# Bucket rows on TensorE for the compressed branch's biases, and a skewed read of a short line for the others

## The chip, the cores and the metric

The kernel runs on one core of a Trainium2 chip. The metric is the device time of one execution in microseconds; three executions of the kernel before took 597.0, 598.36 and 598.94 us, the median being 598.36 us. The engines are named as in the profile: PE (TensorE, with PEld for its weight loads), DVE (VectorE), ACT (ScalarE), POOL (GpSimd) and SP (SyncE, which here only issues DMAs, as SPq).

## The reference

One layer of a decoder block on a sequence of 256 positions with model width 1024: a Conformer convolution module and a sparse attention side by side, one output projection, a cross-attention into 256 memory tokens, a SwiGLU feed-forward, and RMS norms between them. What the change touches are the biases of the sparse attention. It has 16 heads of 64 and three branches: attention over 15 compressed keys (blocks of 32 positions at a stride of 16), over selected blocks, and over a window. All three add to their scores a bias that depends on the distance of query and key alone, by way of 32 buckets and one table of 32 buckets by 16 heads:

```python
dist_c = t[:, None] - c_end[None, :]
bias_c = rel_bias[t5_bucket(dist_c)].reshape(S, n_cmp, G, R).transpose(2, 3, 0, 1)
s_c = jnp.einsum("bsgrd,bngd->bgrsn", qg, k_cmp).astype(jnp.float32) * scale + bias_c
p_cmp = masked_softmax(s_c, dist_c >= 0)
```

where `c_end` of compressed key n is 16n + 31. With 256 positions the selected blocks are all four blocks of the sequence and the window covers everything, so both other branches are plain causal attention over 256 keys, each with its own keys and values, and share one bias of query minus key.

## The kernel before, in words

All weights come through one ring: `half` (L136) takes a tile of the tag "w", which has three buffers of 4 KB in each partition, has SP load 512 KB into it, and `split` (L126) writes a high part (ACT, L129) and a low part (DVE, L131) of it. When both are written, the buffer is free for the next load. A product (`product`, L146) is three matmuls on high and low parts; a `gemm` (L151) is 48 of them on two such loads, into one of two PSUM banks.

The order of the program is: norm and first cross-attention keys, the eight products u0 to u7 of the convolution module, the products kc and vc of the compressed branch, q0 to q3, ks, kw, vs, vw, a small gate product wg, the gates ga0 to ga3, then eight calls of `pair` (L517), one for each two heads, with the products gc0 to gc3 and v0 to v3 as fillers between them, and then output projections, cross-attention and feed-forward.

Beside these run the 31 taps of the depthwise convolution, made at a lower priority (L323 to L330): `taps_g` on ACT and POOL (L317 to L321), `taps_v` on DVE (L304). When they are all there, `layer_norm_sums` (L597) adds them up on POOL, and PE makes the mean `mu` (L604) from that.

The order of instructions within an engine, the place of every DMA in SP's queue and the buffer that a tile takes are settled before the run by a planner, which plays the program through with a model of its own and gives each engine the ready instruction of the highest priority. `tc.issue_after(ins)` adds that the instructions of its block stand behind `ins` in an issue order; it is no wait for `ins` to end.

The biases before: `relt` (L333, a "w" tile) holds the bucket table and, for 383 distances, which bucket each has; one product gives `rel_ps`, a line of 384 bias values (negated) for each head, copied to `rel_sb` (L338, 16 partitions). `table` (L343) writes 8 query rows of `negb`, a table of 16 heads by 128 queries by 256 in DRAM, straight from `rel_sb` by an access that steps back one element for each query. Its 16 calls stand behind the products kc, vc, q0 to q3, ks and kw. `bias_of` (L348) loads two heads of `negb`, 256 KB, into a tile of the tag "nb" (two buffers). It is called eight times for the compressed branch, as `nbc` (L490), and eight times for the pairs, as `nb` (L520).

The compressed branch makes its scores `cs_ps` (L482) in high and low columns, ACT copies the high ones to `nsc` (L485), DVE adds the low ones (L486), sets the columns that no query sees (L488), and adds the biases, every 16th column of each `nbc` tile, in 16 small additions (L493). Minimum, subtraction, exponential (L500, queued behind the sigmoid of ga3), mask, sum and scaling follow, and four transposes (L511). `nsc` is a tile of the tag "pr" (four buffers), which `rel_sb`, `zz` and the pairs' `p1` tiles take too.

`xr` (L688) is a second load of x, 1 MB, for the residual after the output projection at 329 us; its buffer was that of `zin` of the product vc.

Of the kernel before, what the change touches and what calls it, by code (L numbers as in the profile page):

```python
# [25 lines left out]
BUCKETS = 32  # L26
MAX_DIST = 128
EPS = 1e-6
BIG = 1e30
NCMP = 15  # L30
# [27 lines left out]


@with_exitstack  # L60
def tile_hybrid_block(
# [9 lines left out]
    cp: bass.AP,  # L71
    rel: bass.AP,
    out: bass.AP,
):
    nc = tc.nc
# [18 lines left out]
    def small(name, shape, dt=F32, tag=None, bufs=1):  # L94
        return sb.tile(shape, dt, tag=tag or name, name=name, bufs=bufs)
# [4 lines left out]
    def aux(name, shape, tag, bufs):  # L100
        return axp.tile(shape, F32, tag=tag, name=name, bufs=bufs)
# [147 lines left out]
    for at, n in ((0, 2), (2, 2), (4, 2), (6, 2)):  # L249
        hs = slice(at, at + n)  # L250
# [58 lines left out]
    def taps_g(j, begin):  # L309

        y = yt[:, j:j + 2]
        for t in range(begin, TAPS):
# [7 lines left out]
            if t > begin:  # L320
# [11 lines left out]

    relt = small("relt", [P, 512], tag="w", bufs=3)  # L333
    nc.sync.dma_start(relt, rel)
    rel_ps = aux("rel_ps", [P, 384], "s", 2)
    nc.tensor.matmul(rel_ps, lhsT=relt[:, 0:P], rhs=relt[:, P:512],
                     start=True, stop=True)
    rel_sb = small("rel_sb", [HEADS, 384], tag="pr", bufs=4)  # L338
    nc.scalar.activation(rel_sb, rel_ps[:HEADS], AF.Copy)
    negb = drp.tile([HEADS, P, S], F32, name="negb")  # L340
    row = rel_sb[:]

    def table(i):  # L343

        nc.sync.dma_start(negb[:, 8 * i:8 * i + 8], bass.AP(tensor=row.tensor, offset=row.offset + P - 1 - 8 * i,
                                                            ap=[list(row.ap[0]), [-1, 8], [1, S]]))

    def bias_of(hp, name):  # L348

        t = small(f"{name}{hp}", [P, 2, S], tag="nb", bufs=2)  # L350
        nc.sync.dma_start(t, negb[2 * hp:2 * hp + 2].rearrange("h q k -> q h k"))
        return t
# [7 lines left out]
    for kv, name in enumerate(("kc", "vc")):  # L360
        ps = gemm(name, h)
        for i in range(2):
            table(2 * kv + i)
        kc = long(f"{name}t", 11 + 2 * kv, (P, GROUPS, S))
# [47 lines left out]
    for j in range(4):  # L412
        ps = gemm(f"q{j}", h)
        for i in range(2):
            table(4 + 2 * j + i)
# [12 lines left out]
    for br, name in enumerate(("ks", "kw")):  # L428
        ps = gemm(name, h)
        for i in range(2):  # L430
            table(12 + 2 * br + i)
        for lo, g in ((0, 0), (64, 1)):
# [46 lines left out]

    nsc = small("nsc", [P, 2, HEADS, 16], tag="pr", bufs=4)  # L480
    for qb in range(2):
        cs_ps = aux(f"cs_ps{qb}", [P, HEADS, 2, 16], "s", 2)  # L482
        for hd in range(HEADS):
            nc.tensor.matmul(cs_ps[:, hd], lhsT=qh(hd, qb), rhs=kcp[:, hd // 4], start=True, stop=True)
        nc.scalar.activation(nsc[:, qb], cs_ps[:, :, 0], AF.Copy)  # L485
        nc.vector.tensor_tensor(out=nsc[:, qb], in0=cs_ps[:, :, 1], in1=nsc[:, qb], op=ALU.add)  # L486
    for qb, n in ((1, NCMP), (0, 7)):
        nc.vector.memset(nsc[:, qb, :, n:], BIG)  # L488
    for hp in range(8):
        nb = bias_of(hp, "nbc")  # L490
        hs = slice(2 * hp, 2 * hp + 2)
        for qb, off, n in ((1, 31, NCMP), (0, 159, 7)):
            nc.vector.tensor_tensor(out=nsc[:, qb, hs, 0:n], in0=nsc[:, qb, hs, 0:n],  # L493
                                    in1=nb[:, :, off::16][:, :, 0:n], op=ALU.add)
    mc = small("mc", [P, 2, HEADS])
# [21 lines left out]
    def pair(hp):  # L517
        heads = (2 * hp, 2 * hp + 1)
        g = heads[0] // 4
        nbp = bias_of(hp, "nb")  # L520
        s0 = aux(f"s0_{hp}", [P, 2, 2, P], "s0", 1)
# [166 lines left out]
    xr = long("xr", 14)  # L688
    nc.sync.dma_start(xr, xt)
    x1, xg, acc1 = residual(by_halves([f"wo{j}" for j in range(4)], (yh, yl)), xr, PP_GX, "1", (0, 1, 6))  # L690
# [106 lines left out]

def _buckets():

    half = BUCKETS // 2  # L800
    ratio = MAX_DIST // half
    res = []
    for n in range(S):
        if n < half:
            res.append(n)
            continue
        b = half
        while b < BUCKETS - 1 and n ** half >= half ** half * ratio ** (b + 1 - half):
            b += 1
        res.append(b)  # L810
    return res


_OUTS = [((P, NB, S), "float32")]
# [88 lines left out]
```

## Time and profile before

| what | value |
|---|---|
| median of three executions | 598.36 us |
| the profiled execution's own time | 597.25 us |
| its span | 595.5 us |
| granted TensorE clock, mean | 0.984 |
| PE, DVE, ACT, POOL busy | 94%, 75%, 64%, 30% of the span |
| bytes moved by DMA | 101.48 MB |

The span is the time from the first to the last instruction of the profiled execution; the 1.75 us between it and the execution's time lie around it. A row of a timeline holds the start in us, the duration in us, engine, line of the source, operation, tile written and tile read, and a count where several were merged (the duration is then that from the first to the last). "[x <-Y]" at its end says that the engine sat idle x us before it and that Y ended the wait. A row of the view of waits has the waiting engine and instruction, what it waited for, and then the microseconds in total, how often, and the longest. A row of the stretches has start and end, length, and each engine's busy time with its instructions, then the granted clock, the share of time that the DMA engines were busy, and GB/s.

### The profile page before, as it was taken

What the parts mean: (1) busy time and instruction counts of PE and PEld (TensorE: products, weight loads), DVE (VectorE), ACT (ScalarE), POOL (GpSimd) and SP (SyncE); (2) the same over time, 40 slices, a digit from 0 to 9 for tenths busy, and PEclk for the clock granted to TensorE, in tenths of its full rate; (3) what the DMA queues carried; (4) which work ended last, traced back from release to release, by engine and by line L of the source; (5) the groups of instructions that cost most, each with busy time, mean ns of one, the idle gap of its engine ahead of it and who ended that gap; (6) DMA issues with size and microseconds to landing.
All of it is one profiled execution on the core that took longest, in us unless ns stands there. A gap on an engine that the chain in (4) does not pass through costs nothing.

```text
span 595.5 us, 11133 instructions
## 1 busy us (share of the span) xinstructions
PE 561.8 (94%) x4248; PEld 531.5 (89%) x4248; DVE 447.5 (75%) x807; ACT 382.1 (64%) x712; POOL 177.8 (30%) x127
## 2 busy tenths in 40 slices
PE   8999895969899889999999999999999999999995
PEld 7889895969899889888999999998888888899995
DVE  5585798889999999977675957577877877854542
ACT  5557686377775789969844666467666566554440
POOL 0344997688799934000000300041000000000000
PEclk9999999898899999999999999999999999999998
DMA  8755568763577535321355554145556556566631
GB/s 291 244 181 176 197 179 194 200 222 105 147 232 236 194 114 187 123 85 68 126 180 188 180 166 153 66 153 182 204 176 210 179 177 210 177 176 184 191 89 70
DMA packets 34789, 101.48 MB, mean 170 GB/s; under 512 B 3632, under 2 KB 11184, under 8 KB 34480
## 3 DMA queue, kind: packets, MB, share of 16 engines
q1 hardware_dynamic: 33008, 98.67, 51.6%
q10 hardware_dynamic: 1728, 2.10, 1.3%
q8 instruction: 33, 0.54, 0.3%
q14 instruction: 20, 0.16, 0.1%
HBM read 96.56 MB, written 3.15 MB: 167 GB/s over the span
## 4 chain that ended last, share of the span: by engine, by line
PE 64%; DVE 15%; DMA 7%; issue 6%; ACT 5%; POOL 3%; DVEq 0%; SPq 0%; ACTq 0%; POOLq 0%
PE ps_f L745 14%; PE ps_f L747 7%; DVE yp L304 4%; PE fo L149 4%; PE fo L148 4%; PE fo L147 4%; DMA q<-in_wst_dram 3%; DMA k<-in_wst_dram 2%; PE ps_xq L148 1%; PE ps_pw L148 1%; PE ps_xo L148 1%; PE ps_v L149 1%; PE ps_xq L147 1%; PE ps_xq L149 1%; PE ps_xo L147 1%
## 5 line engine op out<-in xcount | busy, mean ns | idle before, releaser
L321 POOL TENSOR_TENSOR yt<-yt,vw 128x512 f32<-128x512 f32 x69 | 113.3, 1643 | 34.0 <-ACT vw L319 29.9
L319 ACT ACTIVATE vw<-vt,ppt 128x256 f32<-128x256 f32 x114 | 51.0, 499 | 23.6 <-POOL yt L321 23.2
L745 PE MATMUL ps_f<-g,f_1h 128*128 128x512 f32 x176 | 47.9, 391 | 0.0
L745 PE MATMUL ps_f<-g,f_0h 128*128 128x512 f32 x176 | 47.7, 394 | 0.0
L304 DVE SCALAR_TENSOR_TENSOR yp<-vt,ppt,yp 128x256 f32<-128x256 f32 x98 | 43.8, 479 | 0.7
L131 DVE TENSOR_TENSOR f_0l<-f,f_0h 128x1024 fp32r<-128x1024 f32 x22 | 27.5, 1249 | 21.9 <-ACT sl L752 21.0
L778 POOL COPY acc<-s 128x256 f32<-128x256 f32 x1 | 0.8, 815 | 134.2 <-ACT s L776 134.2
L745 PEld LDWEIGHTS ps_f<-g,f_1h 128*128 128x128 f32 x176 | 33.0, 188 | 7.5 <-DVE g L680 0.4
L745 PEld LDWEIGHTS ps_f<-g,f_0h 128*128 128x128 f32 x176 | 30.4, 190 | 4.1
L748 ACT ACTIVATE ab<-ps_f 128x256 f32<-128x256 f32 x44 | 16.4, 374 | 23.7 <-PE ps_f L747 23.7
L129 ACT ACTIVATE f_0h<-f 128x1024 fp32r<-128x1024 f32 x22 | 23.3, 1060 | 12.8 <-PE ps_f L745 9.7
L683 POOL COPY acc<-s_wo 128x256 f32<-128x256 f32 x1 | 0.9, 934 | 100.1 <-ACT s_wo L676 100.1
L747 PEld LDWEIGHTS ps_f<-g,f_0l 128*128 128x128 f32 x176 | 26.9, 189 | 3.3
L747 PE MATMUL ps_f<-g,f_1l 128*128 128x256 f32 x176 | 28.4, 283 | 0.0
L747 PE MATMUL ps_f<-g,f_0l 128*128 128x256 f32 x176 | 28.0, 282 | 0.0
L131 DVE TENSOR_TENSOR f_1l<-f,f_1h 128x1024 fp32r<-128x1024 f32 x22 | 26.9, 1221 | 0.7 <-ACT f_1h L129 0.7
L747 PEld LDWEIGHTS ps_f<-g,f_1l 128*128 128x128 f32 x176 | 24.3, 192 | 0.0
L129 ACT ACTIVATE f_1h<-f 128x1024 fp32r<-128x1024 f32 x22 | 23.1, 1049 | 1.2 <-DMA f<-in_wst_dram 1.1
L317 POOL TENSOR_SCALAR vw<-vt,ppt 128x256 f32<-128x256 f32 x24 | 21.5, 907 | 0.8
L147 PE MATMUL ps_u<-hh,u_0h 128*128 128x256 f32 x64 | 18.5, 289 | 2.1 <-DVE vt L288 2.1
L131 DVE TENSOR_TENSOR u_1l<-u,u_1h 128x1024 fp32r<-128x1024 f32 x8 | 14.1, 1765 | 7.3 <-ACT u_1h L129 7.3
L148 PE MATMUL ps_u<-hl,u_0h 128*128 128x256 f32 x64 | 18.2, 284 | 1.3 <-DVE hl L207 1.3
(547 smaller groups left out, 2287.7 us busy)
## 6 DMA issues: line engine op xcount, KB each, us to landing
f<-in_wst_dram SPq DMA_DIRECT2D x44, 512.0 KB, 3.8
fo<-in_wfo_dram SPq DMA_DIRECT2D x20, 512.0 KB, 3.8
u<-in_wst_dram SPq DMA_DIRECT2D x16, 512.0 KB, 4.3
q<-in_wst_dram SPq DMA_DIRECT2D x8, 512.0 KB, 6.3
ga<-in_wst_dram SPq DMA_DIRECT2D x8, 512.0 KB, 4.0
gc<-in_wst_dram SPq DMA_DIRECT2D x8, 512.0 KB, 3.7
v<-in_wst_dram SPq DMA_DIRECT2D x8, 512.0 KB, 3.7
pw<-in_wst_dram SPq DMA_DIRECT2D x8, 512.0 KB, 3.6
```

The source lines that it names most:

```text
L129: nc.scalar.activation(hi, w, AF.Copy)
L131: eng.tensor_tensor(out=lo, in0=w, in1=f(hi[:]), op=ALU.subtract)
L147: nc.tensor.matmul(o, lhsT=wh, rhs=xh, start=start, stop=False)
L148: nc.tensor.matmul(o, lhsT=wh, rhs=xl, start=False, stop=False)
L149: nc.tensor.matmul(o, lhsT=wl, rhs=xh, start=False, stop=stop)
L304: nc.vector.scalar_tensor_tensor(out=yt[:, k] if last else acc[:, i], in0=v, scalar=w, in1=acc[:, i], op0=ALU.mult, op1=ALU.add)
L317: nc.gpsimd.tensor_scalar(out=pr[:, i], in0=v, scalar1=w, scalar2=0.0, op0=ALU.mult, op1=ALU.add)
L319: nc.scalar.activation(pr[:, i], v, AF.Identity, scale=w, bias=col(PP_DB, j + i) if t == 0 else 0.0)
L321: nc.gpsimd.tensor_tensor(out=y, in0=y, in1=pr, op=ALU.add)
L745: nc.tensor.matmul(ps, lhsT=hs[kb // 4][0][:, kb % 4, cs], rhs=fg[:, :, kb], start=kb == 0, stop=False)
L747: nc.tensor.matmul(ps[:, 1], lhsT=hs[kb // 4][1][:, kb % 4, cs], rhs=fg[:, 0, kb], start=False, stop=kb == NB - 1)
L748: nc.scalar.activation(ab[:, b], ps[:, 0], AF.Copy)
```

## The change

Three things change. First, the compressed branch gets its biases from TensorE. The host now also passes `cb` (128 x 4 x 256, 512 KB) and 256 more columns of `rel`. For each compressed key n, `CROWS[n]` rows hold the buckets that this key can meet, and one row more for the mask; the 16 keys are put together in four groups of at most 128 rows (3, 3, 4 and 6 keys; `CGROUPS`). In `cb`, each query has a -1 in the row of its bucket or the mask value in the mask row; in the added columns of `rel` stand the biases of those rows. Eight products, four groups by two query halves, give all biases of the compressed branch, with sign and mask, in one PSUM bank `cb_ps`; ACT copies them to `nsc`, whose tile is now taken at this place, and later DVE adds the high and the low scores to it. The 16 small additions, the two memsets, the copy of the high scores and the eight loads of `nbc` are gone.

Second, the table `negb` and its 16 writes are gone. The line `rel_sb` is written once to DRAM, eight times over for each head (`line`, 16 x 8 x 384, 196 KB). `bias_of` reads a head's 128 x 256 biases from it skewed: sixteen partitions to a copy, each starting one element before the last. That is two DMAs of 128 KB for a pair in place of one of 256 KB.

Third, the load of `xr` is put into an `issue_after(mark)` block; `mark` is at that place what the last call of `pair` returned, a matmul of pair 7.

```diff
+def _groups():
+    far = [S - 1 - (16 * n + 31) for n in range(16)]
+    rows = [(_buckets()[d] + 1 if d >= 0 else 0) + 1 for d in far]
+    groups, n = [], 0
+    while n < 16:
+        m = n
+        while m < 16 and sum(rows[n:m + 1]) <= P:
+            m += 1
+        groups.append(list(range(n, m)))
+        n = m
+    return rows, groups
+CROWS, CGROUPS = _groups()
+RT_CB = 512
+RT_END = RT_CB + 16 * HEADS
...
-    relt = small("relt", [P, 512], tag="w", bufs=3)
+    relt = small("relt", [P, RT_END], tag="w", bufs=3)
     nc.sync.dma_start(relt, rel)
+    cbt = small("cbt", [P, len(CGROUPS), S], tag="w", bufs=3)
+    nc.sync.dma_start(cbt, cb)
     rel_ps = aux("rel_ps", [P, 384], "s", 2)
     nc.tensor.matmul(rel_ps, lhsT=relt[:, 0:P], rhs=relt[:, P:512],
                      start=True, stop=True)
+    nsc = small("nsc", [P, 2, HEADS, 16], tag="pr", bufs=4)
+    cb_ps = aux("cb_ps", [P, 2, 16, HEADS], "s", 2)
+    for qb in range(2):
+        for i, ns in enumerate(CGROUPS):
+            n0, n1 = ns[0], ns[-1] + 1
+            nc.tensor.matmul(cb_ps[:, qb, n0:n1].rearrange("p n h -> p (n h)"), lhsT=cbt[:, i, qb * P:qb * P + P],
+                             rhs=relt[:, RT_CB + 16 * n0:RT_CB + 16 * n1], start=True, stop=True)
+    nc.scalar.activation(nsc, cb_ps.rearrange("p q n h -> p q h n"), AF.Copy)
     rel_sb = small("rel_sb", [HEADS, 384], tag="pr", bufs=4)
     nc.scalar.activation(rel_sb, rel_ps[:HEADS], AF.Copy)
-    negb = drp.tile([HEADS, P, S], F32, name="negb")
-    row = rel_sb[:]
-    def table(i):
-        nc.sync.dma_start(negb[:, 8 * i:8 * i + 8], bass.AP(tensor=row.tensor, offset=row.offset + P - 1 - 8 * i,
-                                                            ap=[list(row.ap[0]), [-1, 8], [1, S]]))
-    def bias_of(hp, name):
-        t = small(f"{name}{hp}", [P, 2, S], tag="nb", bufs=2)
-        nc.sync.dma_start(t, negb[2 * hp:2 * hp + 2].rearrange("h q k -> q h k"))
+    line = drp.tile([HEADS, 8, 384], F32, name="line")
+    nc.sync.dma_start(line, rel_sb.unsqueeze(1).to_broadcast([HEADS, 8, 384]))
+    row = line[:]
+    def bias_of(hp):
+        t = small(f"nb{hp}", [P, 2, S], tag="nb", bufs=2)
+        for k in range(2):
+            nc.sync.dma_start(t[:, k], bass.AP(tensor=row.tensor, offset=row.offset + 8 * 384 * (2 * hp + k) + P - 1,
+                                               ap=[[384 - 16, 8], [-1, 16], [1, S]]))
         return t
...
     (behind the products kc, vc, q0 to q3, ks, kw: the calls of table are gone)
...
-    nsc = small("nsc", [P, 2, HEADS, 16], tag="pr", bufs=4)
...
-        nc.scalar.activation(nsc[:, qb], cs_ps[:, :, 0], AF.Copy)
-        nc.vector.tensor_tensor(out=nsc[:, qb], in0=cs_ps[:, :, 1], in1=nsc[:, qb], op=ALU.add)
-    for qb, n in ((1, NCMP), (0, 7)):
-        nc.vector.memset(nsc[:, qb, :, n:], BIG)
-    for hp in range(8):
-        nb = bias_of(hp, "nbc")
-        hs = slice(2 * hp, 2 * hp + 2)
-        for qb, off, n in ((1, 31, NCMP), (0, 159, 7)):
-            nc.vector.tensor_tensor(out=nsc[:, qb, hs, 0:n], in0=nsc[:, qb, hs, 0:n],
-                                    in1=nb[:, :, off::16][:, :, 0:n], op=ALU.add)
+        for i in range(2):
+            nc.vector.tensor_tensor(out=nsc[:, qb], in0=cs_ps[:, :, i], in1=nsc[:, qb], op=ALU.add)
...
     xr = long("xr", 14)
-    nc.sync.dma_start(xr, xt)
+    with tc.issue_after(mark):
+        nc.sync.dma_start(xr, xt)
```

More of the change, by code (lines that the diff above doesn't have):

```diff
@@ L57, with _buckets @@
 CP_END = CP_HM + 8
+def _buckets():
+    half = BUCKETS // 2
+    ratio = MAX_DIST // half
+    res = []
+    for n in range(S):
+        if n < half:
+            res.append(n)
+            continue
+        b = half
+        while b < BUCKETS - 1 and n ** half >= half ** half * ratio ** (b + 1 - half):
+            b += 1
+        res.append(b)
+    return res
+def _groups():
[12 more added lines that the diff above has]
+RT_END = RT_CB + 16 * HEADS
 @with_exitstack
@@ L72, in tile_hybrid_block @@
     rel: bass.AP,
+    cb: bass.AP,
     out: bass.AP,
@@ L361, in tile_hybrid_block @@
         ps = gemm(name, h)
-        for i in range(2):
-            table(2 * kv + i)
         kc = long(f"{name}t", 11 + 2 * kv, (P, GROUPS, S))
@@ L429, in tile_hybrid_block @@
         ps = gemm(name, h)
-        for i in range(2):
-            table(12 + 2 * br + i)
         for lo, g in ((0, 0), (64, 1)):
@@ L795, in tile_hybrid_block @@
         nc.sync.dma_start(out[:, ks], x3[:, ks])
[L798 to L811, printed above, removed]
 _OUTS = [((P, NB, S), "float32")]
@@ L883 @@
             rel[BUCKETS, P + i] = BIG
+    cb = _np.zeros((P, len(CGROUPS), S), x["x"].dtype)
+    for i, ns in enumerate(CGROUPS):
+        at = 0
+        for n in ns:
+            mask = at + CROWS[n] - 1
+            rel[at:mask, RT_CB + HEADS * n:RT_CB + HEADS * n + HEADS] = x["rel_bias"][:CROWS[n] - 1]
+            rel[mask, RT_CB + HEADS * n:RT_CB + HEADS * n + HEADS] = 1.0
+            for q in range(S):
+                d = q - (16 * n + 31)
+                if n < NCMP and d >= 0:
+                    cb[at + bucket[d], i, q] = -1.0
+                else:
+                    cb[mask, i, q] = BIG
+            at = mask + 1
     ins = {
         "xt": rows(x["x"][0].T), "memt": rows(x["mem"][0].T), "wst": wst, "wgn": _np.concatenate([win[:, :, 4608:4656], _np.zeros((P, NB, P - 48), win.dtype)], axis=2),
-        "wfo": wfo, "w1": w1, "pp": pp, "cp": cp, "rel": rel,
+        "wfo": wfo, "w1": w1, "pp": pp, "cp": cp, "rel": rel, "cb": cb,
     }
```

6 lines of the change are left out of this document (2 added, 4 removed).

## The prediction

> **What bounds the kernel now.** I read the page of the profile first (busy shares and span, told above), then stretches, then who waits for whom, then SP's own order.
>
> ```profile
> core 0: us, PE busy (x) PEld busy (x) DVE busy (x) ACT busy (x) POOL busy (x), PEclk, DMA share, GB/s
> 78.00:92.00 14.00, 12.60 (x100) 11.86 (x98) 13.43 (x19) 11.02 (x22) 13.43 (x10) 1.00 0.78 183
> 92.00:110.00 18.00, 12.95 (x84) 12.65 (x84) 14.32 (x22) 9.39 (x17) 11.57 (x9) 0.81 0.89 212
> 110.00:131.00 21.00, 18.18 (x176) 17.32 (x176) 18.11 (x27) 15.02 (x33) 16.35 (x12) 1.00 0.62 211
> 131.00:165.00 34.00, 28.64 (x212) 28.16 (x211) 32.95 (x52) 24.79 (x49) 27.17 (x22) 0.90 0.44 137
> 165.00:205.00 40.00, 37.91 (x309) 37.14 (x308) 39.93 (x69) 26.24 (x46) 38.50 (x27) 1.00 0.70 222
> 205.00:240.00 35.00, 32.04 (x248) 30.05 (x247) 33.54 (x108) 30.56 (x77) 15.70 (x10) 1.00 0.44 149
> 240.00:523.00 283.00, 282.55 (x2035) 259.83 (x2035) 210.87 (x401) 186.71 (x355) 15.53 (x16) 1.00 0.48 159
> ```
>
> From 240 to 523 us PE is busy 282.55 of 283 us: nothing the change does there can help, and only a wait could hurt. Everything is decided between 78 and 240 us. Two limits follow one another. From 92 to 131 us nobody is full (DVE idles 39 - 32.43 = 6.6 us, PE 7.9 us and at a clock of 0.81 in the first part), while the DMA engines are at 0.89. From 131 to 205 us DVE is full: 72.88 of 74 us, with PE idle for 7.4 us.
>
> ```profile
> ACT q_1h L129 <- DMA q<-in_wst_dram: 10.4, 3, 4.8
> POOL yt L321 <- ACT vw L319: 10.2, 4, 4.9
> DVE q_1l L131 <- ACT q_1h L129: 4.6, 3, 2.3
> SPq L351 <- DMA negb<-rel_sb: 4.1, 1, 4.1
> q<-in_wst_dram SPq DMA_DIRECT2D x8, 512.0 KB, 6.3
> u<-in_wst_dram SPq DMA_DIRECT2D x16, 512.0 KB, 4.3
> negb<-rel_sb SPq DMA_DIRECT2D x16, 128.0 KB, 5.3
> 106.33 1.66 SPq L345 DMA_DIRECT2D negb<-rel_sb  x1
> 112.27 0.91 SPq L351 DMA_DIRECT2D nbc<-negb  x2
> 113.23 0.93 SPq L139 DMA_DIRECT2D q<-in_wst_dram  x2
> ```
>
> The first four rows are waits between 92 and 131 us. The chain is plain: the q loads land late, ACT waits 10.4 us for them, and behind ACT wait DVE's low parts and POOL's taps. Why are they late? A load of 512 KB takes 4.3 us among the u products and 6.3 us here, where the 16 table writes (2 MB) share the queue; and at 108 us SP itself stands still for 4.1 us, because the first `nbc` load must wait for the last table write, with two q loads queued behind it. They leave together at 113.23 us.
>
> **The change part by part.** *DVE, 166 to 190 us.* Gone are 16 additions and two memsets; two PSUM additions of the kind of L486 come in for ACT's copies.
>
> ```profile
> L493 DVE TENSOR_TENSOR nsc<-nsc,nbc 128x14 f32<-128x14 f32 (+1 forms) x16 | 5.0, 364 | 0.0
> L488 DVE MEMSET nsc<- 128x144 f32 (+1 forms) x2 | 0.2, 125 | 0.0
> L486 DVE TENSOR_TENSOR nsc<-cs_ps,nsc 128x256 f32<-128x256 f32 x2 | 0.7, 409 | 0.0
> L485 ACT ACTIVATE nsc<-cs_ps x2: 378/380/383, 162.9 to 163.2; 128x256 f32<-128x256 f32 x2
> ```
>
> 5.0 + 0.2 - 2 x 0.41 = 4.4 us less, in a stretch where DVE has 0.07 us of idle time in 40. I count it in full: -4.4 us. Bounds: 0 (another engine was as late) to -4.4. ACT trades two copies (0.76 us) for one of 512 elements at about the same price: 0.
>
> *The q stage, 92 to 131 us.* Table writes, two `nbc` loads and the stand at 108 us go. What can be won is what DVE idled, at most 6.6 us, since from 131 us on DVE carries the time; at least 0, if DVE's fixed order finds the next late thing. What is late next is DVE itself, with its low parts and taps. I take 4.0 us, nearer to the upper end because the DMA rows explain ACT's 10.4 us: -4.0 us.
>
> *The ring, 76 to 95 us.* This is the cost. `cbt` takes a buffer of the ring, and `relt` cannot leave before the new products have read both.
>
> ```profile
> 71.42 0.33 SPq L334 DMA_DIRECT2D relt<-in_rel_dram  x1
> 75.94 2.58 SPq L139 DMA_DIRECT2D kc<-in_wst_dram  x2
> 78.87 4.65 SPq L139 DMA_DIRECT2D vc<-in_wst_dram  x2
> 78.19 4.89 DMA kc<-in_wst_dram
> 83.11 1.07 ACT kc_1h L129
> 84.20 2.13 DVE kc_1l L131
> 90.27 1.92 DVE L131 TENSOR_TENSOR vc_1l<-vc,vc_1h 128x1024 fp32r<-128x1024 f32 x1
> L336 PE MATMUL rel_ps<-relt x2: 483/485/487, 78.0 to 78.4; 128*128 128x384 f32 x2
> L380 PE MATMUL z_ps<-zin,w1t x64: 222/222/270, 110.0 to 119.9; 128*64 128x64 f32 x64
> ```
>
> Today the four loads kc and vc leave at 75.94, 78.19, 78.87 and 83.19 us. With `cbt` in the buffer that comes free at 75.94, kc_0 leaves at 78.19, and kc_1 only when kc_0 is split: 78.19 + 4.89 + 1.07 + 2.13 = 86.3 us, 8.1 us later than now; vc_0 and vc_1 about then too (7.4 and 3.1 us later). Played on at 4.3 us a load and 2.4 to 3.2 us a split, kc_1 is split at 94 us and vc_1 at some 96.5 us, 4 us behind today's 92.2. From 94 us on the q loads can leave, and three buffers that each come free after 4.3 + 3 us let one leave every 2.4 us: the sixth at 106 us, where it leaves at 113.23 today. So the loss has a place to be won back, but ACT, DVE and POOL starve in it; DVE can do taps (L304) meanwhile, as far as the planner puts them there. Bounds: 0 (all filled with taps) to +8.1; I take the middle of what DVE sees, the 4 us at vc_1 less half a microsecond for taps: +3.5 us.
>
> *Products and copy.* Eight products of 48 to 96 columns, two matmuls each: at 0.22 to 0.48 us a matmul by L380 and L336, 16 of them, overlapped, are 2 to 4 us of PE while it waits for kc_1 anyway: 0; at most +4 if the planner puts them ahead of u7. ACT's copy waits for them, `rel_sb` and the `line` write stand behind it, and the first pair loads behind that on SP: one more stand of at most a write's 5.3 us, at a time when the ring has no free buffer to load: 0. `nsc` holds a "pr" buffer from 86 us on, but `rel_sb` and `zz` are done long before the pairs, which find three free, as now: 0.
>
> *The pair loads.* Two DMAs of 128 KB instead of one of 256 KB, each issue at some 0.4 us.
>
> ```profile
> nb<-negb SPq DMA_DIRECT2D x8, 256.0 KB, 3.1
> 261.21 0.38 SPq L351 DMA_DIRECT2D nb<-negb  x1
> 271.10 0.41 DVE L533 CUSTOM_DVE_ANT_0 p<-s,nb 128x256 f32<-128x256 f32 x1
> ```
>
> The last pair's load has 9.9 us from issue to use and takes 3.1 us; were both halves in series, 6.2 us still fit. Cover: the two buffers. Price 0, and 3.1 us for each pair if the cover were gone. [...]
>
> *`xr`.* Its 6.6 us landing beside the ks loads could go.
>
> ```profile
> 122.33 0.42 SPq L689 DMA_DIRECT2D xr<-in_xt_dram  x1
> 189.49 0.34 SPq L139 DMA_DIRECT2D gc<-in_wst_dram  x1
> L529 PE MATMUL s<-kdh,qt x2: 278/282/285, 202.5 to 203.2; 128*128 128x256 f32 x2
> ```
>
> But gc0 stands in a block behind pair 0's `mark`, a PE matmul (L529, 202.5 us and on), and its loads left from 189.49 us. So such a block holds back only instructions of the mark's own engine; SP's are not held, and `xr` should stay near 122 us. 0 either way: a sooner ks load meets a full DVE from 131 us on.
>
> Sum: -4.4 - 4.0 + 3.5 = -4.9 us. The profiled execution took 597.25 us, 1.1 us below the median, and would take 592.4; on the median's level 598.36 - 4.9 = 593.5 us.
>
> **The rivals.** *A, slower: the ring starves and nothing comes back.* If the planner has few taps ready for the gap, the 8.1 us reach DVE and PE, and the q stage then runs at DVE's pace without winning: +8.1 - 4.4 = +3.7, 602.1 us. It decides from the point where the loss at kc exceeds 8.4 us less what the q stage wins. For it: kc_1l follows its load, and PE's next product follows that, with no spare buffer; and DVE is already busy 13.43 of 14 us there. Against: the loads ahead by q2.
>
> *B, no change: POOL holds the gain.* PE waits for POOL's sums once:
>
> ```profile
> PE mu L604 <- POOL ysum L215: 1.6, 1, 1.6
> L321 POOL TENSOR_TENSOR yt<-yt,vw 128x512 f32<-128x512 f32 x69 | 113.3, 1643 | 34.0 <-ACT vw L319 29.9
> L317 POOL TENSOR_SCALAR vw<-vt,ppt 128x256 f32<-128x256 f32 x24 | 21.5, 907 | 0.8
> ```
>
> POOL's taps are 134.8 us of work ahead of `mu`. If POOL doesn't come forward, `mu` comes when it comes now, and PE, early, waits 1.6 + 4.9 us: 598.4. Against: POOL lost 10.2 us waiting for ACT in the q stage, for the same loads.
>
> *C, more: all of DVE's idle time and no loss at kc*: -4.4 - 6.6 = -11, 587.4 us. Against: the ring's arithmetic.
>
> *D, `xr` does move*: as the forecast, within 1 us, with the ks loads sooner. Evidence against is above; 1 in 10, inside the other cases.
>
> **How the numbers follow.** A measurement here tells about 0.3%, 1.8 us, from no change. Forecast (-1.8 to -8 us): 0.44. A: 0.32. B: 0.14. C: 0.10. Faster is forecast plus C, 0.54; same is B, 0.14; slower is A, 0.32. The range goes from C's 587.4 down to 587.0, and up to A's 602.1 and a little over, 603.0 (A with part of the PE products uncovered); I leave some 0.04 below and 0.12 above. The forecast's own range is 590.4 to 596.5.
>
> **What would show it.** Right: no SP stand at 108 us, q loads landing in about 4.3 us, the clock of that stretch near 1.00, DVE's idle time there below 3 us, kc_1 leaving near 86 us, `mu` some 5 us earlier. Wrong: gaps of DVE and POOL between 84 and 96 us that no taps fill, a longer wait of `mu` for POOL, or an SP stand of the first pair loads behind `line` with weight loads behind them.

## The result, and the profile after

The changed kernel took 594.03 us (median of four executions, 593.57 to 594.53) against 598.53 us of the kernel before (597.0 to 598.94): a ratio of 0.992, with an interval of 0.9891 to 0.9949. That is faster by some 4.5 us, where 4.9 were forecast. The profiled execution took 593.57 us, with a span of 591.8 us and a mean granted clock of 0.984; 98.13 MB were moved by DMA, 3.35 MB less. The sum came out, in part by luck: of its terms only some did, as the experiments show.

The same stretches as in the prediction, in the kernel after (columns as there; the last ends at 518 us, since what follows comes some 4 us earlier):

```profile
78.00:92.00 14.00, 11.53 (x90) 10.78 (x90) 12.19 (x24) 9.77 (x21) 12.62 (x10) 0.98 0.54 180
92.00:110.00 18.00, 18.00 (x154) 17.64 (x153) 17.75 (x24) 14.36 (x25) 16.85 (x12) 0.92 0.64 189
110.00:131.00 21.00, 16.32 (x143) 15.29 (x142) 20.75 (x30) 15.10 (x33) 19.73 (x14) 1.00 0.55 181
131.00:165.00 34.00, 32.39 (x261) 31.59 (x262) 32.71 (x52) 26.22 (x49) 29.33 (x22) 1.00 0.55 168
165.00:205.00 40.00, 33.08 (x255) 31.43 (x254) 37.54 (x71) 36.68 (x69) 34.82 (x25) 0.95 0.40 130
205.00:240.00 35.00, 34.80 (x274) 33.14 (x273) 31.70 (x91) 29.16 (x71) 8.39 (x6) 0.96 0.48 160
240.00:518.00 278.00, 277.55 (x1998) 255.93 (x1996) 206.29 (x388) 179.88 (x333) 15.53 (x16) 1.00 0.49 161
```

From 92 to 131 us DVE idles for 0.5 us in 39, where it idled for 6.6, and the DMA engines are down from 0.89 to 0.64 in the first part. But from 165 to 205 us something new stands there: PE idles for 6.9 us in 40 (before: 2.1), and ACT's busy time has gone from 26.24 to 36.68 us.

Who waits in the q stage, by the view of waits from 84 to 131 us, and SP's own row from the same view of its queue:

```profile
POOL yt L359 <- ACT vw L357: 2.1, 3, 0.9
ACT q_0h L167 <- DMA q<-in_wst_dram: 0.6, 1, 0.6
SPq L390 <- ACT rel_sb L388: 0.4, 1, 0.4
ACT vw L357 <- POOL yt L359: 10.7, 8, 2.6
```

ACT waits 0.6 us for the q loads instead of 10.4, and POOL 2.1 us for ACT instead of 10.2. The longest wait is now one of ACT for POOL's taps, 10.7 us (before: 2.7), with POOL busy for 36.58 of the 39 us from 92 to 131 us. SP stands for 0.4 us at the write of `line`; the stand of 4.1 us at 108 us is gone. The order in which SP issues, from its timeline in the kernel after, and one row of the kernel before that answers to it:

```profile
85.29 0.33 SPq L177 DMA_DIRECT2D kc<-in_wst_dram  x1
92.17 0.68 SPq L390 DMA_DIRECT2D line<-rel_sb  x1
97.26 1.96 SPq L397 DMA_DIRECT2D nb<-line  x3
99.75 0.61 SPq L397 DMA_DIRECT2D nb<-line  x1
121.77 0.42 SPq L722 DMA_DIRECT2D xr<-in_xt_dram  x1
```

```profile
189.93 0.90 SPq L351 DMA_DIRECT2D nb<-negb  x2
```

`kc_1` leaves at 85.29 us and `xr` at 121.77 us, both about where the prediction put them. What it did not put anywhere is the third and fourth row: the loads for pairs 0 and 1 leave at 97 to 100 us. In the kernel before, the first of them left at 189.93 us, because the eight `nbc` loads used the same two buffers of the tag "nb" until then. So pair 0 could not start before; now it can, and the planner lets it, in the middle of the gate stage. ACT's timeline of the kernel after shows what comes with that (`p` is a tile of a pair, L567 and L574 its exponentials, L495 and L508 sigmoids; a row without names is the load of the table of functions):

```profile
167.28 1.28 ACT L567 ACT_TABLE_LOAD   x1
...
174.62 1.28 ACT L495 ACT_TABLE_LOAD   x1
...
176.20 0.90 ACT L357 ACTIVATE vw<-vt,ppt 128x256 f32<-128x256 f32 x2
177.11 1.28 ACT L567 ACT_TABLE_LOAD   x1
178.41 0.51 ACT L567 ACTIVATE p<-p,mins 128x256 f32<-128x256 f32 x1
```

Between 165 and 205 us there are seven such loads (167.28, 174.62, 177.11, 184.01, 190.69, 197.16 and 201.29 us) of 1.28 us each, one for every turn from exponential to sigmoid or back; the kernel before has its first one after 150 us at 207.01 us. On DVE, in the same stage:

```profile
194.68 1.36 DVE L584 TENSOR_SCALAR p<-p,sums 128x256 f32<-128x256 f32 x1
...
199.87 1.29 DVE L586 TENSOR_SCALAR p<-p,sums 128x128 f32<-128x128 f32 x1
...
201.47 1.91 DVE L169 TENSOR_TENSOR gc_0l<-gc,gc_0h 128x1024 fp32r<-128x1024 f32 x1
```

Eight scalings of pair 0 (the first and the last are shown, from 194.68 us to 201.16 us) stand ahead of `gc_0l` in DVE's order, though its high part `gc_0h` was written at 195.4 us. PE's timeline has the bill:

```profile
199.10 0.38 PE L185 MATMUL ps_gc<-hh,gc_0h 128*128 128x256 f32 x1 [1.37 <-ACT sga L508]
...
203.43 0.58 PE L187 MATMUL ps_gc<-hh,gc_0l 128*128 128x256 f32 x1 [3.83 <-DVE gc_0l L169]
203.81 0.41 PE L185 MATMUL ps_gc<-hh,gc_0h 128*128 128x256 f32 x1
...
207.62 0.28 PE L185 MATMUL ps_gc<-hh,gc_1h 128*128 128x256 f32 x1
```

PE stands still for 3.83 us; after that a matmul starts every 0.21 us until 207.62 us, and every 0.12 us from there on. Nineteen matmuls take 4.2 us instead of 2.3. Of PE's 6.9 us of idle time between 165 and 205 us 3.8 are this stall, 2.7 are two waits for sigmoids that stand behind a table load (`sgn`, 1.35 us at 176.35 us, and `sga`, 1.37 us at 199.10 us), and 0.4 are short waits.

Where the time was won and lost can be followed by PE's products, since all kernels run them in the same order. A row gives the shortest, the median and the longest duration in ns, and then the first and the last start in us; the first fence is the kernel before, the second the kernel after.

```profile
L147 PE MATMUL ps_q<-hh,q_0h x32: 278/283/551, 103.1 to 137.4; 128*128 128x256 f32 x32
L147 PE MATMUL ps_ks<-hh,ks_0h x8: 283/349/554, 143.5 to 148.8; 128*128 128x256 f32 x8
L147 PE MATMUL ps_ga<-hh,ga_0h x32: 278/283/384, 176.0 to 200.5; 128*128 128x256 f32 x32
L147 PE MATMUL ps_pw<-z,pw_0h x32: 278/283/468, 289.8 to 313.5; 128*128 128x256 f32 x32
```

```profile
L185 PE MATMUL ps_q<-hh,q_0h x32: 278/283/357, 103.0 to 135.6; 128*128 128x256 f32 x32
L185 PE MATMUL ps_ks<-hh,ks_0h x8: 283/283/359, 140.7 to 144.7; 128*128 128x256 f32 x8
L185 PE MATMUL ps_ga<-hh,ga_0h x32: 283/283/385, 169.5 to 195.8; 128*128 128x256 f32 x32
L185 PE MATMUL ps_pw<-z,pw_0h x32: 283/283/283, 284.0 to 309.8; 128*128 128x256 f32 x32
L636 PE MATMUL mu<-ysum,ones x2: 377/378/378, 212.9 to 213.1; 128*128 128x256 f32 x2
```

PE is level at the first q product (103.0), 2.8 us ahead at ks, 6.5 us at the first gate product, 4.7 us at the last. `mu` comes at 212.9 us, 2.5 us earlier than the 215.4 us of before, and the last product of the output projection 3.7 us earlier. Each row comes from one execution: the first table load behind 150 us stands at 167.28 us in the kernel after and at 169.35 us in the same kernel with `xr` loaded late (below), whose time is the same (594.03 and 594.18 us). A lead of a microsecond or two says little by itself.

### The profile page after: what moved, and what is told of

The parts are those of the page before. It is cut to its first block, busy times and chain, and to the rows that moved or that the text cites. A ratio compares the mean times of both kernels' runs of the same rounds, so it can differ in the third digit from the quotient of the medians.

```text
span 591.8 us, 11124 instructions
## 1 busy us (share of the span) xinstructions
PE 561.9 (95%) x4264; PEld 532.1 (90%) x4264; DVE 445.0 (75%) x791; ACT 390.4 (66%) x717; POOL 172.8 (29%) x127
## 2 busy tenths in 40 slices
DMA packets 30597, 98.13 MB, mean 166 GB/s; under 512 B 3280, under 2 KB 6864, under 8 KB 30288
## 4 chain that ended last, share of the span: by engine, by line
PE 67%; DVE 12%; ACT 7%; issue 5%; DMA 4%; POOL 4%; ACTq 0%; DVEq 0%; SPq 0%; POOLq 0%
PE ps_f L778 14%; PE ps_f L780 7%; PE fo L187 4%; PE fo L186 4%; PE fo L185 4%; DVE yp L342 3%; POOL yt L359 3%; DMA k<-in_wst_dram 3%; ACT vw L357 2%; PE ps_gc L187 1%; PE ps_xq L186 1%; PE ps_gc L185 1%; PE ps_gc L186 1%; PE ps_pw L185 1%; PE ps_xo L186 1%
## 5 line engine op out<-in xcount | busy, mean ns | idle before, releaser
L167 ACT ACTIVATE f_0h<-f 128x1024 fp32r<-128x1024 f32 x22 | 23.3, 1059 | 13.3 <-PE ps_f L778 10.2
L782 DVE TENSOR_TENSOR ab<-ps_f,ab 128x256 f32<-128x256 f32 x44 | 18.4, 419 | 0.7 <-ACT ab L781 0.7
```

What stands on the lines that cost most here:

```text
L167: nc.scalar.activation(hi, w, AF.Copy)
L782: nc.vector.tensor_tensor(out=ab[:, b], in0=ps[:, 1], in1=ab[:, b], op=ALU.add)
```

## The experiments

My theory after the result: the q stage and DVE won about what was forecast or more; the early pair 0 takes part of it back; the ring costs little. The rivals: the early pair only moves work and costs nothing; the ring is what takes it back; one of the two halves of the change does all of it alone. Ratios are to the kernel before, run beside each, with intervals of 95%; they are not the quotients of the medians. The kernel before had a median of 597.94 us beside rows 2 to 5, 598.76 beside rows 6 to 9, and 598.81 beside rows 10 to 13.

| kernel | median us | ratio | interval |
|---|---|---|---|
| after | 594.03 | 0.992 | 0.9891 to 0.9949 |
| after, pairs' exponentials behind ga3 | 590.52 | 0.9857 | 0.9831 to 0.9883 |
| after, `relt` and `cbt` outside the ring | 592.96 | 0.990 | 0.9872 to 0.9927 |
| biases from PE only | 598.51 | 1.0007 | 0.9984 to 1.0029 |
| line only | 598.18 | 0.9984 | 0.996 to 1.0007 |
| line only, 8 narrow additions in place of 16 | 594.2 | 0.993 | 0.9912 to 0.9948 |
| before, `nbc` in buffers of its own | 601.7 | 1.006 | 1.0038 to 1.0083 |
| after, `xr` late | 594.18 | 0.9932 | 0.9913 to 0.9951 |
| after, exponentials late and no `cbt` in the ring | 594.43 | 0.9932 | 0.9914 to 0.9949 |
| after, again | 593.46 | 0.9914 | 0.9892 to 0.9936 |
| exponentials behind ga3, again | 591.31 | 0.9873 | 0.9854 to 0.9891 |
| after, line kept 16 times | 594.24 | 0.9926 | 0.9908 to 0.9944 |
| exponentials behind ga3, and more taps on DVE | 590.18 | 0.9863 | 0.9839 to 0.9887 |

**Is it the early pair?** The exponentials of all pairs are put behind the sigmoid of ga3 in ACT's order; scores and minima of pair 0 stay free to come early.

```diff
     for j in range(4):
         mark = gate(f"ga{j}", sga[:, 2 * j:2 * j + 2], AF.Sigmoid)
+    gated = mark
...
-                exp1 = nc.scalar.activation(p1[k][:, br], p1[k][:, br], AF.Exp, scale=-1.0, bias=mins[:, hd, 1, br:br + 1],
-                                            accum_out=sums[:, hd, 1, br:br + 1])
+                with tc.issue_after(gated):
+                    exp1 = nc.scalar.activation(p1[k][:, br], p1[k][:, br], AF.Exp, scale=-1.0, bias=mins[:, hd, 1, br:br + 1],
+                                                accum_out=sums[:, hd, 1, br:br + 1])
...
     (the same for exp)
```

> The changed kernel, with the exponentials of the pairs queued on ACT behind the sigmoid of ga3. Theory 1: the changed kernel starts pair 0 inside the gate stage, because its biases are there by 101 us and no nbc load holds the two nb buffers any more; each turn between exponential and sigmoid costs ACT a table load of 1.28 us, and pair 0's scalings stand ahead of gc0's low part on DVE (PE waits 3.8 us). Then the table loads between 150 and 310 us fall from 11 to 5 or 6, PE's idle time between 165 and 205 us from 6.9 to about 2 us, and the time from 594.0 to about 590. Rival: that idle time comes from DVE's and ACT's taps, which are as many as before; then 594 stays within 1 us. Second rival: with the exponentials late, the pairs come late and the fillers run out; then 595 to 597.

It took 590.52 us (0.9857). In the tile views of this kernel:

```profile
L185 PE MATMUL ps_ga<-hh,ga_0h x32: 283/283/297, 169.7 to 192.8; 128*128 128x256 f32 x32
L639 PE MATMUL mu<-ysum,ones x2: 379/431/483, 207.5 to 207.8; 128*128 128x256 f32 x2
L185 PE MATMUL ps_pw<-z,pw_0h x32: 278/283/363, 280.7 to 306.5; 128*128 128x256 f32 x32
```

The gates start at the same time as in the kernel after (169.7 and 169.5 us) and end 3.0 us sooner; `mu` comes 5.4 us sooner, and the last output projection 3.3 us. Some 2 of the 5.4 us are given back between those two places; the exponentials, too, have to be made at some time. Both kernels were run once more, beside each other:

> The changed kernel as it is, beside the next three on one chip: 0.992 of the kernel before, as measured, within 0.3%.

> The changed kernel with the exponentials behind ga3 once more, now directly beside the changed kernel. If the early pair costs what the first run says, 0.986 of before and 3 to 4 us under the changed kernel; if that run owed something to its chip or hour, less than 2 us under it.

593.46 against 591.31 us: 2.2 us between the medians, where the profiles had 3.3 and the first two medians (594.03 and 590.52) 3.5. So the early pair costs the changed kernel 2 to 4 us; the second pair of runs stands at the lower end, under the 3 to 4 us that the first one had led me to expect. The edit removes the table loads and, with the exponentials, the scalings ahead of `gc_0l`. By the rows above, 3.0 of the 5.4 us at `mu` are lost within the gates, and 2.4 between the last gate product and `mu`, where the stall at `gc_0l` stands. The table loads alone need not cost much: the next kernel but one, with `cbt` outside the ring, has five of them from 165 to 205 us and no wait at `gc_0l`, and PE idles for 1.0 us in these 40.

**Is it the buffers?** In the kernel before, `nbc` gets four buffers of its own, so that the "nb" buffers are free for the pairs; nothing else is changed.

```diff
+    nbcs = long("nbcs", 13, (P, 4, 2, S))
     for hp in range(8):
-        nb = bias_of(hp, "nbc")
+        nb = nbcs[:, hp % 4]
+        nc.sync.dma_start(nb, negb[2 * hp:2 * hp + 2].rearrange("h q k -> q h k"))
```

> The kernel before with one change: nbc in a long buffer that is free at that time, four tiles at once, so that the two nb buffers are free for the pairs from the start. Theory 1: this alone makes the plan start pair 0 inside the gate stage, with four to six more table loads on ACT before 205 us (five between 150 and 310 us now), PE idles more between 165 and 205 us (2.1 us now), and the time rises to 600 to 602. Rival: the early pair is harmless without the rest of the change; then 597 to 599.

It was slower, 1.006. Its ACT timeline has, from 190 to 250 us, nine table loads where the kernel before has three; the first is

```profile
194.82 1.28 ACT L537 ACT_TABLE_LOAD   x1
```

So the buffers alone bring the early pair, in a kernel with neither `cbt` nor `line`, and this kernel is 0.6%, about 3.6 us, slower. That all of it is the pair's price is argued, not shown: the loads of `nbc` change their places too, and this kernel with late exponentials was not run. The other kernels agree: wherever no `nbc` holds the "nb" buffers and the exponentials are free (after, `cbt` outside the ring, biases from PE only, `xr` late, 16 copies), the first table load behind 150 us lies between 167 and 175 us; where `nbc` is kept in them (before, both line-only kernels) it lies at 203 to 207 us.

**What does the ring cost?** `relt` and `cbt` get places of their own, and their loads are queued behind the last weight load ahead of them.

```diff
-    relt = small("relt", [P, RT_END], tag="w", bufs=3)
-    nc.sync.dma_start(relt, rel)
-    cbt = small("cbt", [P, len(CGROUPS), S], tag="w", bufs=3)
-    nc.sync.dma_start(cbt, cb)
+    relt = long("relt", 13, (P, RT_END))
+    cbt = long("cbt", 12, (P, len(CGROUPS), S))
+    with tc.issue_after(loads[-1]):
+        nc.sync.dma_start(relt, rel)
+        nc.sync.dma_start(cbt, cb)
```

> The changed kernel, with relt and cbt in two long buffers that are free at that time, so that the weight ring keeps its three buffers. Theory 1: the ring costs what the prediction said, 3.5 us: kc_1 leaves at 78 to 79 us instead of 85.3, PE ends kc by 92 us instead of 97.2, and the time falls to about 590.5. Rival: DVE filled the gap with taps and is the limit afterwards; then kc ends as early, but the time stays within 1 us of 594.

592.96 us (0.990); the interval overlaps that of the kernel after. Its tile views, and then its waits:

```profile
L185 PE MATMUL ps_kc<-hh,kc_0h x8: 278/283/366, 88.5 to 92.6; 128*128 128x256 f32 x8
L185 PE MATMUL ps_q<-hh,q_0h x32: 279/283/551, 103.4 to 134.4; 128*128 128x256 f32 x32
```

```profile
PE ps_q L185 <- DVE kct L414: 3.1, 1, 3.1
PE ps_vs L185 <- DVE kdl L477: 2.3, 1, 2.3
```

The last rows of kc come 2.7 us sooner than after (92.6 and 95.3 us), but the first q product starts at 103.4 us, not sooner than 103.0: PE waits 3.1 us there for DVE's copies `kct`. In the kernel before, with a ring without `cbt`, it started at 103.1 us, too. So what `cbt` delays is a time in which PE would have waited at q0 anyway; the price there is nil, and at the end 1.1 us by the medians, with overlapping intervals; the 590.5 us of a ring that costs 3.5 us were not reached.

The end is no clean price, though, for the two kernels part again behind ks. The gates start at 173.0 us here, 3.5 us behind the kernel after, and PE waits 2.3 us for DVE's `kdl` ahead of vs (second row). The kernel before has that wait too (2.5 us), both line-only kernels have 1.4 us of it. With `cbt` in the ring, PE waits 0.5 us for `kdl` in the kernel after and not at all with late exponentials, in whose view the shortest wait has 0.2 us; with the biases from PE only the wait is not among those of 0.9 us or more. PE's lead over the kernel before grows from 2.8 to 6.5 us between ks and the first gate product in the kernel after, and falls from 3.4 to 3.0 us in this one. So an order of DVE that is worth some 3.6 us there goes with `cbt` in the ring. Whether the ring brings it about or the planner hit on it by chance is not shown.

**Each half alone.** First the biases from PE, with the table, its writes and the loads of pairs as before:

```diff
-    line = drp.tile([HEADS, 8, 384], F32, name="line")
-    nc.sync.dma_start(line, rel_sb.unsqueeze(1).to_broadcast([HEADS, 8, 384]))
+    negb = drp.tile([HEADS, P, S], F32, name="negb")
...
     (table and its 16 calls, and bias_of reading negb, as in the kernel before)
```

> Only the first part of the change: the compressed branch's biases from TensorE, the pairs' biases still from the table of 16 writes. Theory 1: DVE's 4.4 us are saved, the ring loss of about 3.5 us stays, the q loads stay late behind the table writes (6 us and more to land) and pair 0 starts early as its two buffers are free: 597 to 600, no clear gain over before. Rival: DVE's work is what counts; then 594 to 595, as the whole change.

598.51 us, no change (1.0007). The q loads are late again and the early pair is there, so this run does not price DVE's relief by itself; its waits from 84 to 131 us:

```profile
DVE q_1l L169 <- ACT q_1h L167: 4.6, 1, 4.6
ACT q_1h L167 <- DMA q<-in_wst_dram: 4.2, 2, 3.8
```

Then the line alone: `negb` and its writes gone, `nbc` and its additions kept and read from `line`.

```diff
-    negb = drp.tile([HEADS, P, S], F32, name="negb")
...
+    line = drp.tile([HEADS, 8, 384], F32, name="line")
+    nc.sync.dma_start(line, rel_sb.unsqueeze(1).to_broadcast([HEADS, 8, 384]))
...
     (bias_of reads line, for nbc and nb; the calls of table are gone)
```

> Only the second part: the line kept eight times and the skewed reads, for the compressed branch (nbc) and the pairs alike; no cb, no ring loss, DVE's 16 additions stay, and nbc still holds the two nb buffers until 185 us. Theory 1: the q stage wins all it can (DVE idled 6.6 us there), pair 0 is not early, so 592 to 593, better than the whole change. Rival: the gain is in DVE's additions and the q stage's gain is taken by DVE later; then 597 to 598.

598.18 us, no change either (0.9984): my theory for this run fell. The stage itself did what was forecast, and more was lost behind it. Its last stretch before 240 us, its tile views and its waits:

```profile
205.00:240.00 35.00, 30.94 (x222) 29.45 (x221) 30.88 (x105) 29.62 (x80) 13.31 (x9) 0.90 0.44 143
```

```profile
L147 PE MATMUL ps_ks<-hh,ks_0h x8: 280/363/552, 139.5 to 145.8; 128*128 128x256 f32 x8
L147 PE MATMUL ps_pw<-z,pw_0h x32: 278/283/363, 288.4 to 314.2; 128*128 128x256 f32 x32
```

```profile
PE ps_ga L149 <- DVE ga_1l L131: 3.4, 3, 1.5
PE mu L596 <- POOL ysum L215: 2.4, 1, 2.4
```

ks starts at 139.5 us, 4.0 us ahead of the kernel before. In the gate stage PE then waits 3.4 us for DVE's low parts (before: 1.9), `mu` waits 2.4 us for POOL's sums (before: 1.6) and the next product that needs such sums, `rn_l`, 1.4 us (before: 0.5), PE idles 4.1 us between 205 and 240 us at a clock of 0.90 (before: 3.0 at 1.00), and the last output projection is 0.7 us behind the kernel before. So the lead is lost where PE waits for DVE and POOL. To take DVE's additions away as well, eight of the 16 are dropped and the other eight get one column for each head; this kernel leaves out the biases of all other columns:

```diff
-        for qb, off, n in ((1, 31, NCMP), (0, 159, 7)):
+        for qb, off, n in ((1, 31, 1),):
```

> The line alone, as before, and of the 16 additions of compressed biases only eight, of one column each (so the biases of all other columns are left out and the compressed branch is computed wrongly); loads, buffers and order of nbc stay. It takes some 4.2 us of DVE work away and nothing else. Theory 2: the q stage's gain and DVE's work are two limits on the same path (taps, sums, mu), and each part alone is covered by the other; then the line with DVE's work taken away gives 590.5 to 592, as the whole change with late exponentials does, since it has no early pair either. Rival: the line's gain is lost for another reason (fillers, POOL); then 596 to 598.

594.2 us (0.993), 0.54% or some 3.2 us below the line alone, and the intervals do not touch. But it did not take the 4.2 us from DVE that it was meant to. The additions in the line-only kernel, and here:

```profile
L485 DVE TENSOR_TENSOR nsc<-nsc,nbc 128x14 f32<-128x14 f32 (+1 forms) x16 | 5.9, 412 | 1.2 <-DMA nbc<-line 1.2
L485 DVE TENSOR_TENSOR nsc<-nsc,nbc 128x2 f32<-128x2 f32 x8 | 4.7, 596 | 1.4 <-DMA nbc<-line 1.4
```

It is 1.2 us less, and in the gates PE waits longer for DVE's low parts than with the line alone (5.9 us against 3.4). What is gone are the waits for POOL's sums behind the gates: 0.3 us in place of 2.4 and 1.4. That is 3.5 us, about the difference of the two kernels; which part of the new order brings POOL's sums in time was not followed up. The time also missed the 590.5 to 592 us that I expected: it is 3 us or more above late exponentials, so something else in the change wins as well. What is shown is that neither half won anything by itself (+0.0007 and -0.0016, with 1 inside both intervals) and that together they win 0.8%; that DVE's relief is what carries the line's lead to the end is argued.

**The small parts.** `xr` in its new place does not move, as was seen above. To learn what moving it would bring, its block is put behind the last weight load, which does move it:

```diff
-    with tc.issue_after(mark):
+    with tc.issue_after(loads[-1]):
```

> The changed kernel with the load of xr queued behind SP's last weight load of that place in the program instead of behind a matmul; SP then issues it behind the eight loads of pw, near 280 us, in place of 122 us, and nothing else moves. All theories: the ks load issued behind it lands sooner by up to 2 us, DVE is the limit there, and the time stays within 1 us of 594.0; that the third part of the change is worth nothing is then shown both ways. If 592 or less, the ks stage hangs on that load.

It leaves at 298.64 us, and the time is 594.18 us (0.9932): the same. To learn whether the time depends on how many copies the pair loads read, the line is kept 16 times:

```diff
-    line = drp.tile([HEADS, 8, 384], F32, name="line")
+    line = drp.tile([HEADS, 16, 384], F32, name="line")
...
-                                               ap=[[384 - 16, 8], [-1, 16], [1, S]]))
+                                               ap=[[384 - 8, 16], [-1, 8], [1, S]]))
```

> The changed kernel with the line kept sixteen times and eight partitions to a copy, so that the slowest dimension of each pair load is 16 and not 8. The plan of the engines should be nearly the same. If the pair loads are hidden, as the prediction said, the time stays within 1 us of the changed kernel, whatever the eight copies cost the loads; if they hold up the pairs, it falls by 2 us or more.

594.24 us beside 593.46 of the kernel after: the same.

**Better versions.** Both mends together, late exponentials and no `cbt` in the ring, with the two diffs shown above:

> The changed kernel with exponentials behind ga3 and relt and cbt outside the weight ring, both. Alone they took it from 594.0 to 590.5 and to 593.0. If the two losses are apart: 589 to 590. If DVE is the limit behind the ring, as the second alone suggests: 590 to 591, no better than the first alone.

594.43 us (0.9932), worse than late exponentials alone, whose intervals (0.9831 to 0.9883 and 0.9854 to 0.9891) it does not touch, and no better than `cbt` outside the ring with the exponentials free (592.96 us, 0.990, with overlapping intervals). Where the ring is free, then, no cost of the early pair is seen. It is level at ks (140.3 us, 140.8 with late exponentials alone) and behind from the gates on, by its waits and its tile view:

```profile
PE ps_vs L185 <- DVE kdl L477: 2.5, 1, 2.5
```

```profile
L185 PE MATMUL ps_ga<-hh,ga_0h x32: 281/283/385, 173.3 to 197.3; 128*128 128x256 f32 x32
```

The gates start at 173.3 us, 3.6 us behind the 169.7 of late exponentials alone, after a wait of 2.5 us for DVE's `kdl` that the other kernel does not have; it is the wait that was seen above in all kernels without `cbt` in the ring. Why the planner's order of DVE comes out so much worse with a freer ring was not followed up; this stays open. Last, late exponentials with more of the taps on DVE, in case POOL's sums are the next limit:

```diff
-SHARE = 21
+SHARE = 23
```

> The kernel with late exponentials, and two taps of the last block moved from POOL to DVE (21 of 31 taps to 23). There DVE idles 4.9 us between 165 and 205 us, POOL 1.2, and PE waits 2.1 us for POOL's sums at mu. If POOL's taps are the limit that is left, 588 to 590; if DVE is, 592 and more.

590.18 us (0.9863), between the two ranges expected, and not told apart from late exponentials without it. Late exponentials, some 590.5 to 591.3 us, are the best version found, better than both kernels.

## Why the prediction was right, and where it was not

*DVE, -4.4 us: the work went, its worth is not shown.* The additions and memsets are gone as counted, but DVE's busy time over the whole span fell by 2.5 us only (447.5 to 445.0). "I count it in full" rested on DVE's 0.07 us of idle time in 40, and no run prices it: the kernel with the biases from PE only has the early pair and late q loads with it, and the narrow additions took 1.2 us from DVE, not 4.2. In the gates, where the additions stood, PE's lead over the kernel before grows by 1.4 us with late exponentials (from 6.3 to 7.7) and shrinks by 1.8 in the changed kernel.

*The q stage, -4.0 us: right in its place, but not by itself.* The mechanism was as told: no stand of SP, no wait of ACT for loads. The q loads landed in 4.9 us at the median (3.6 to 6.2), not quite the 4.3 forecast, where it was 6.3. DVE's idle time there is 0.5 us (below 3 was forecast), and PE is 2.8 us ahead at ks, 4.0 in the line-only kernel. What is late next is not DVE alone, as I wrote, but POOL's taps too (ACT's 10.7 us). And the worth at the end is 1 us or nothing when the line is alone. The sum added it to the DVE term as if the two were independent; alone, the halves win nothing. The clock of 92 to 110 us was 0.92, not "near 1.00".

*The ring, +3.5 us: wrong in size.* `kc_1` left at 85.29 us, and I had 86.3; kc and vc came later, as played on. The sixth q load left at 109.7 us, where I had 106. The failing step is "I take the middle of what DVE sees". The lower bound was the right one at that place: what counted was the first q product, which starts at 103.0 to 103.7 us in the profiles of before, after, line only and both kernels without `cbt` in the ring, and where PE comes early to it (`cbt` outside the ring) it waits 3.1 us there for DVE's copies `kct`. What no term has are the 3.7 us that PE gains between ks and the first gate product, with the wait for `kdl` gone.

*The pair loads, "Cover: the two buffers. Price 0": this is the step that failed.* I costed only whether the loads might come too late: they do not, for ahead of its 64 operations on `nb` in the kernel after DVE idles 0.2 us in all, and that for PE, and with 16 copies the time stays the same (594.24 and 593.46 us). The trace of the kernel after lists no landing time for these loads, so how long one takes is not shown, nor what the number of copies does to that. What I missed is that the two buffers were held by `nbc` until 189.93 us, in a row that I could have read, and that without it pair 0 comes early, into a stage whose ACT makes sigmoids and whose DVE was full: its first exponential stands at 168.58 us, where it stood at 208.85. Price: +2 to +4 us in this kernel.

So -4.4 - 4.0 + 3.5 came out at -4.9 partly by luck, with a loss in it that did not occur and without one that did, of about the same size. The measured terms do not make up the measured -4.5. By place, PE is 2.8 us ahead at ks, 6.5 at the first gate product, 4.7 at the last, 2.5 at `mu` and 3.7 at the last product of the output projection, which is the difference of the two profiled executions; the largest step, 3.7 us, is in no term. By times at the end, the line alone wins about 1.0 us, not told apart from nothing, and the early pair costs 2.2 to 3.5, so that the biases from PE, with the order that comes with them, would have to win 5.7 to 7.0 us beside the line; without the line they win nothing, with the early pair in it. How that gain divides between DVE's work, the order of DVE ahead of vs and POOL's sums stays open.

*`xr`, 0: right*, in its place (121.77 us) and in its worth (nothing, even when it does move).

*`mu` "some 5 us earlier": 2.5 us.* PE reached it late by the stall at `gc_0l`; with late exponentials it comes 7.9 us earlier.

*The rivals.* A did not occur: DVE filled the gap (12.19 of 14 us from 78 to 92 us, 17.75 of the next 18), and PE starts the first q product at 103.0 us, where it started at 103.1. Its turning point is misstated, too: by the sum, the loss at kc has to exceed 4.4 us plus what the q stage wins, 8.4 us with the 4.0 counted. B's mechanism is seen in the line-only kernel, where PE waits 3.8 us for POOL's sums at `mu` and `rn_l` (before: 2.1). In the changed kernel PE does not wait for POOL at `mu` at all, because it comes there late itself; with late exponentials it waits 2.1 us. C's part without a loss at kc was true for the first q product, but the early pair stood in its way; late exponentials (590.52 and 591.31 us) are about half the way to its 587.4.

## What to carry to other kernels

When a change frees a buffer, ask not only what could come late, but what may now come early, and which engines it meets there: here an attention pair moved from behind the gates into the midst of them, and ACT changed tables seven times. Two gains on one path aren't to be added without a test of each alone, for either may be worth nothing until the other is made: here neither half won anything alone, and together they won 0.8%. Look in the trace, also, whether an experiment took away what it was meant to: eight additions of two elements took 4.7 us, and 16 of up to 30 took 5.9. And a delay need not cost its length: here the last rows of kc came 2.7 us later with `cbt` in the ring than without, and the first q product no later (103.0 and 103.4 us), since without it PE waited 3.1 us there for `kct`. Look for what else is waited for at the next place before pricing a delay.

## What the runs showed of the hardware that was not expected

Each of the seven turns of ACT between exponential and sigmoid from 165 to 205 us in the kernel after costs a table load of 1.28 us. For the one at 177.11 us it is 1.31 us from the end of the activation ahead (177.10 us) to the start of the next (178.41 us), and 0.02 us of these lie between load and activation.

After PE's stall of 3.83 us the next matmuls came every 0.21 us instead of 0.12 for 4.2 us, which makes the stall 1.9 us dearer than its own length (19 matmuls in 4.2 us, where 19 at 0.12 us are 2.3). A shorter stall was followed by the same. The kernel before has one of 2.50 us, after which a matmul starts every 0.21 us until 163.4 us, for 3.3 us:

```profile
160.06 0.54 PE L147 MATMUL ps_vs<-vs_0h,hh 128*128 128x256 f32 x1 [2.50 <-DVE kdl L435]
```

And two waits of one length, 3.1 us ahead of the first q product, were not followed alike. With `cbt` outside the ring, 2.7 us lie between the first q matmul on `q_0h` and the first on `q_1h`, twelve matmuls later (103.4 and 106.1 us), and the granted clock from 92 to 110 us is 0.81; with both mends it is 1.5 us (103.7 and 105.2 us) at 1.00. So in these traces the length of a stall does not decide this by itself.

An issue of a skewed pair load took SP longer than one of the plain load: 0.59 us for 128 KB, twice for a pair, against 0.38 us for the 256 KB of before. The row is the one of the `nb` tile in the kernel after:

```profile
L397 SPq DMA_DIRECT2D nb<-line x16: 577/592/692, 97.3 to 256.7; - x16
```
